# A hybrid encoder layer on one core: the first microseconds reworked (weights on ScalarE's DMA queue, low parts last, two token blocks open)

## The chip, the core and the metric

The kernel runs on one core of a Trainium2 chip. A core has TensorE (PE; its weight loads are shown apart as PEld), VectorE (DVE), ScalarE (ACT), GpSimd (POOL) and SyncE (SP). Each takes its instructions in the order in which the program lists them. SP issues transfers between the chip's main memory and the core; ACT can issue some too, on a queue of its own. Matmul results land in PSUM, everything else lives in SBUF. The metric is the time of one execution in microseconds (us) of the device, the median of several runs.

## The reference, cut to what matters

One layer for 512 tokens of width 1024, float32. Every projection is taken from the normalised input `h`:

```python
def rmsnorm(x, w):
    y = x * rsqrt(mean(x * x, axis=-1) + EPS)
    return y * w

h = rmsnorm(x, norm_w)                      # (512, 1024)
proj = h @ w_in + b_in                      # (1024, 11272) weights
(mq, mk, mv, mi, mf, mo, mz, sq, sk, sv, sz, gates) = split(proj)
y_m = mlstm(conv(mq, mk), mv, mi, mf) ...   # matrix memory, 4 heads
y_s = stick_breaking(norm(sq), norm(sk), sv) * silu(sz)   # 8 heads
merged = g_m * (y_m @ w_proj_m) + g_s * (y_s @ w_proj_s)
out = x + merged @ w_out
```

The change touches only how `h` and the first 512 columns of `sq` come about.

## The kernel before, in words

**Products in two parts.** To keep float32 accuracy, each operand of a matmul is split into a high part (rounded to the type `fp32r`) and a low part (what is left). A product is three matmuls: high x high, low x high, high x low (`mm3`). `hh` and `hl` are the high and low part of `h`, turned so that the model dimension lies on the partitions: eight k blocks of 128 rows, each with 512 tokens.

**Units.** The weights are worked off in units of 512 KB, 24 matmuls of 512 columns each. A unit is loaded by SP (`load`), split by ACT (high) and DVE (low), multiplied on PE and evacuated. The main loop over `c` (at the end of the code) writes out, for each unit, when later units are loaded and split (`ahead`), and between the two halves of a unit's matmuls the next piece of work of the attention heads. The order in which the program lists the instructions is the order on each engine; nothing reorders them.

**The first four units** (`sq`, 512 columns) are special. Unit i brings rows 256 i to 256 i + 255 of the weights, two k blocks. Their high parts `fh` (`f_w[k][0]`) and low parts `fl` (`f_w[k][1]`) for all eight k are made up front (`first_split`), and what the loop calls the matmuls of unit tb is the product of token block tb (128 tokens) with all eight k: 24 matmuls into one PSUM tile `f_ps[tb]`.

**The beginning.** SP issues, in this order: block 0 of x in two halves (`load_x(0)`), `norm_w`, the weights of units 0 and 1, block 1 of x, the weights of units 2 and 3, blocks 2 and 3 of x, and then many small rows (`load_vecs`). PE meanwhile multiplies zeros (`warm`, tile `idle`). `norm_vec` turns `norm_w`. `x_scale(tb)` squares a block on ACT with a running sum, makes the reciprocal root on POOL (a multiply-add and a power), and scales the block on DVE. `x_turn(tb)` transposes its eight 128 x 128 pieces on PE, four to a PSUM tile; DVE then makes `hh` (one instruction for four pieces) and `hl` (four instructions) from each tile. `first_split(0)` stands ahead of `x_turn(0)`, the splits of units 1 to 3 behind it; the low parts of units 1 and 3 are POOL's, those of 0 and 2 DVE's. In the loop, `x_turn(1)` and `x_turn(2)` stand between the halves of blocks 0 and 1, and `x_turn(3)` behind those of block 1. The evacuation of block tb (`qraw`, DVE) is at the start of step tb + 1, with four Squares on ACT behind it. Unit 4 is the first ordinary one; its first matmul has line 85.

Of the kernel before, what the change touches and what calls it, by code (L numbers as in the profile page):

```python
# [34 lines left out]
def tile_hybrid_layer(  # L35
# [58 lines left out]
    class Unit:  # L94
# [12 lines left out]
        def load(self, tag="stg"):  # L107
            self.st = blk(tag, shape=self.shape)
            nc.sync.dma_start(self.st, self.ap)
# [153 lines left out]
    def x_scale(tb):  # L263
        xs = tiny.tile([128, 4], F32, name="xs", bufs=2)
        ssq, r = xs[:, 0:2], xs[:, 2:3]
        xn = x_t[tb]
        junk = blk("om", BF, (D,), name="junk")
        if tb == 0:
            for i in range(2):
                c = slice(i * D // 2, (i + 1) * D // 2)  # L270
                nc.scalar.activation(junk[:, c], xn[:, c], AF.Square, accum_out=ssq[:, i:i + 1])
            nc.gpsimd.tensor_tensor(ssq[:, 0:1], ssq[:, 0:1], ssq[:, 1:2], op=OP.add)
        else:
            nc.scalar.activation(junk, xn, AF.Square, accum_out=ssq[:, 0:1])
        rstd(r, ssq[:, 0:1], D, EPS)
        nc.vector.tensor_scalar(xn, xn, r, None, op0=OP.mult)

    def x_turn(tb):
        ts = slice(tb * 128, (tb + 1) * 128)
        xn = x_t[tb]  # L280
        for g in range(2):
            ks = slice(4 * g, 4 * g + 4)
            tp = att_ps()
            for j in range(4):
                kt = g * 4 + j
                nc.tensor.transpose(tp[:, j * 128:(j + 1) * 128], xn[:, kt * 128:(kt + 1) * 128], ident)
            dh = hh[:, ks, ts]
            nc.vector.tensor_tensor(dh, tp.rearrange("p (k t) -> p k t", k=4),
                                    nw_t[:, ks].unsqueeze(2).to_broadcast([128, 4, 128]), op=OP.mult)
            for j in range(4):  # L290
                k = 4 * g + j
                nc.vector.scalar_tensor_tensor(hl[:, k, ts], tp[:, j * 128:(j + 1) * 128], nw_t[:, k:k + 1],
                                               hh[:, k, ts].bitcast(F32), op0=OP.mult, op1=OP.subtract)
# [592 lines left out]
    def first_split(i, low=None):  # L886
        u = units[i]
        for j in range(2):
            hi, lo = blk("qk", FR, name="fh"), blk("y", FR, name="fl")
            nc.scalar.activation(hi, u.st[:, j, :], AF.Copy)  # L890
            (low or nc.vector).tensor_tensor(lo, u.st[:, j, :], hi.bitcast(F32), op=OP.subtract)  # L891
            f_w.append((hi, lo))

    units[0].load()
    units[1].load()
# [16 lines left out]
    warm(9)  # L912
    norm_vec()
    x_scale(0)
    warm(2)
    first_split(0)
    x_turn(0)
    first_split(1, nc.gpsimd)
    x_scale(1)
    first_split(2)  # L920
    first_split(3, nc.gpsimd)

    f_ps = []

    def first_mm(tb):
        def mm(half):
            if half == 0:
                f_ps.append(dense_ps())
            for k in range(4 * half, 4 * half + 4):
                sh, sl = h_sta(k, tb)  # L930
                wh, wl = f_w[k]
                nc.tensor.matmul(f_ps[tb], sh, wh, start=k == 0, stop=False)  # L932
                nc.tensor.matmul(f_ps[tb], sl, wh, start=False, stop=False)  # L933
                nc.tensor.matmul(f_ps[tb], sh, wl, start=False, stop=k == KT - 1)  # L934
        return mm
# [44 lines left out]
    for c in range(N):  # L980
# [13 lines left out]
        if c < 2:  # L994
            x_turn(c + 1)
        if c == 0:
            x_scale(2)
            x_scale(3)
# [13 lines left out]
        if c == 1:  # L1012
            x_turn(3)
# [31 lines left out]
```

## Time and profile before

| | |
|---|---|
| median of 3 runs | 719.03 us (718.92 to 719.14) |
| the profiled execution | 720.13 us |
| its span, first to last instruction | 718.4 us |
| PE busy | 709.8 us, 99% of the span |
| DVE, ACT, POOL busy | 424.5, 315.8, 93.5 us |
| mean granted TensorE clock | 0.997 |

The profile shows one execution. Times in it count from the first instruction. Busy time of PE includes the modelled end of each pipelined matmul, so neighbours overlap in the list: of two matmuls that follow one another, the distance of the starts is the time that one takes. "Idle before" is the time an engine stood still ahead of an instruction, and the name behind the arrow is what ended it.

### The profile page before, as it was taken

To read this page: it belongs to the slowest core of one execution; us is meant where nothing else is said; L and a number is where in the kernel's file an instruction comes from. 1 tells how busy PE (TensorE), PEld (TensorE's weight loads), DVE (VectorE), ACT (ScalarE), POOL (GpSimd) and SP (SyncE) were. 2 spreads that over 40 slices of the span, in tenths; PEclk is the share of its full clock that TensorE was granted. 3 is DMA by queue.
4 is the path that set the end of the run, shared out by engine and by line. 5 is a ranking of instruction groups with operands and counts; after the bars stand their busy time and mean duration, and the time that the engine had idled before them with its cause. 6 is when DMAs were issued, how large, how long until landed. Compare 5 with 4: busy or idle time off the path is not lost.

```text
span 718.4 us, 9058 instructions
## 1 busy us (share of the span) xinstructions
PE 709.8 (99%) x3356; PEld 593.1 (83%) x3356; DVE 424.5 (59%) x663; ACT 315.8 (44%) x601; POOL 93.5 (13%) x235
## 2 busy tenths in 40 slices
PE   7999999999999999999999999999999999999997
PEld 5888888888888888888888888888888888888886
DVE  5837886656487568279944737994343254556441
ACT  5245364476255544244475534447554343222210
POOL 5422022253022112000001110000112000000000
PEclk9999999999999999999999999999999999999999
DMA  6433332233323222333332233333223333333621
GB/s 239 133 103 81 109 86 77 69 95 92 99 62 87 58 86 62 102 91 97 101 94 59 63 99 88 91 100 89 74 59 89 89 91 97 104 88 89 234 89 58
DMA packets 91475, 67.80 MB, mean 94 GB/s; under 512 B 3470, under 2 KB 77608, under 8 KB 91432
## 3 DMA queue, kind: packets, MB, share of 16 engines
q1 hardware_dynamic: 91432, 67.23, 32.8%
q8 instruction: 26, 0.43, 0.2%
q14 instruction: 17, 0.14, 0.1%
HBM read 65.12 MB, written 2.10 MB: 94 GB/s over the span
## 4 chain that ended last, share of the span: by engine, by line
PE 97%; DMA 1%; DVE 1%; POOL 0%; SPq 0%; issue 0%; ACT 0%; DVEq 0%
PE dps L85 28%; PE dps L87 27%; PE dps L86 27%; PE aps L86 2%; PE aps L87 2%; PE aps L85 2%; PE aps L440 1%; PE aps L382 1%; DMA stg<-in_w_in_dram 1%; PE dps L934 1%; PE dps L932 1%; PE dps L933 1%; PE aps L735 1%; PE aps L736 1%; PE aps L737 1%; DVE fl L891 0%
## 5 line engine op out<-in xcount | busy, mean ns | idle before, releaser
L91 DVE TENSOR_TENSOR wl<-stg,wh 128x1024 fp32r<-128x1024 f32 x108 | 132.3, 1225 | 140.3 <-ACT wh L90 139.9
L85 PE MATMUL dps<-hh,wh 128*128 128x512 f32 x448 | 175.8, 392 | 0.0
L86 PE MATMUL dps<-hl,wh 128*128 128x512 f32 x448 | 174.6, 390 | 0.0
L87 PE MATMUL dps<-hh,wl 128*128 128x512 f32 x448 | 174.6, 390 | 0.0
L90 ACT ACTIVATE wh<-stg 128x1024 fp32r<-128x1024 f32 x108 | 113.6, 1052 | 95.3 <-PE dps L87 58.6
L87 PEld LDWEIGHTS dps<-hh,wl 128*128 128x128 f32 x448 | 84.1, 188 | 17.7
L85 PEld LDWEIGHTS dps<-hh,wh 128*128 128x128 f32 x448 | 84.2, 188 | 17.5 <-issue 1.0
L86 PEld LDWEIGHTS dps<-hl,wh 128*128 128x128 f32 x448 | 84.2, 188 | 16.6
L85 PE MATMUL dps<-wh,hh 128*128 128x512 f32 x224 | 88.3, 394 | 0.0
L87 PE MATMUL dps<-wh,hl 128*128 128x512 f32 x224 | 87.4, 390 | 0.0
L86 PE MATMUL dps<-wl,hh 128*128 128x512 f32 x224 | 87.4, 390 | 0.0
L87 PEld LDWEIGHTS dps<-wh,hl 128*128 128x128 f32 x224 | 42.1, 188 | 8.9
L86 PEld LDWEIGHTS dps<-wl,hh 128*128 128x128 f32 x224 | 42.1, 188 | 8.2
L85 PEld LDWEIGHTS dps<-wh,hh 128*128 128x128 f32 x224 | 42.1, 188 | 8.2
L626 DVE SCALAR_TENSOR_TENSOR acc<-tmp,vec,acc 128x511 f32<-128x511 f32 (+2 forms) x48 | 36.0, 750 | 1.7
L629 ACT ACTIVATE tmp<-acc 128x512 f32<-128x512 f32 x16 | 10.1, 633 | 50.2 <-DVE acc L626 50.2
L415 DVE TENSOR_TENSOR_SCAN om<-om 128x512 f32<-128x512 f32 (+3 forms) x32 | 27.9, 871 | 6.3 <-POOL om L409 6.3
L409 POOL TENSOR_SCALAR_AFFINE_SELECT om<-om 128x128 f32<-128x128 f32 x32 | 12.1, 378 | 134.5 <-ACT om L407 134.5
L90 ACT ACTIVATE at_split<-aps 128x384 fp32r<-128x384 f32 (+1 forms) x24 | 11.8, 525 | 36.8 <-PE aps L440 36.8
L688 POOL TENSOR_SCALAR_AFFINE_SELECT w_all<-om 128x128 f32<-128x128 f32 x16 | 4.1, 293 | 168.9 <-DVE om L683 168.9
L91 DVE TENSOR_TENSOR at_split<-aps,at_split 128x384 fp32r<-128x384 f32 (+1 forms) x24 | 13.7, 599 | 19.8 <-ACT at_split L90 19.8
L86 PE MATMUL dps<-wl,mgh 128*128 128x512 f32 x64 | 24.9, 389 | 0.0
(239 smaller groups left out, 1170.6 us busy)
## 6 DMA issues: line engine op xcount, KB each, us to landing
stg<-in_w_in_dram SPq DMA_DIRECT2D x87, 512.0 KB, 3.7
stg<-in_w_proj_s_dram SPq DMA_DIRECT2D x8, 512.0 KB, 3.7
stg<-in_w_proj_m_dram SPq DMA_DIRECT2D x8, 512.0 KB, 3.6
stg<-in_w_out_dram SPq DMA_DIRECT2D x8, 512.0 KB, 3.7
brow<-in_b_in_dram SPq DMA_DIRECT2D x8, 256.0 KB, 4.2
xr<-in_x_dram SPq DMA_DIRECT2D x8, 256.0 KB, 5.7
out_dram<-xr SPq DMA_DIRECT2D x7, 256.0 KB, 2.3
x<-in_x_dram SPq DMA_DIRECT2D x3, 512.0 KB
```

Of the source, the lines that this page charges most:

```text
L85: nc.tensor.matmul(ps, ah, bh, start=first, stop=False)
L86: nc.tensor.matmul(ps, ah, bl, start=False, stop=False)
L87: nc.tensor.matmul(ps, al, bh, start=False, stop=last)
L90: nc.scalar.activation(hi, src, AF.Copy)
L91: nc.vector.tensor_tensor(lo, src, hi.bitcast(F32), op=OP.subtract)
L382: nc.tensor.transpose(tp[:, tb * 128:(tb + 1) * 128], self.raw[name][tb][:, hs], ident)
L409: nc.gpsimd.affine_select(out=om[:, ts], in_=om[:, ts], compare_op=OP.is_gt, fill=1.0, base=0, channel_multiplier=1, pattern=[[-1, 128]])
L415: nc.vector.tensor_tensor_scan(back, back, back, 1.0, op0=OP.mult, op1=OP.bypass)
L440: nc.tensor.transpose(tp[:, at + (i - j) * 128:at + (i - j + 1) * 128], a_t[i][:, j * 128:(j + 1) * 128], ident)
L626: nc.vector.scalar_tensor_tensor(acc[:, j:], t[:, 0:T - j], cw(3 - j, ch), acc[:, j:], op0=OP.mult, op1=OP.add)
L629: nc.scalar.activation(t, acc, AF.Sigmoid)
L735: nc.tensor.matmul(nm[:, 0:258], ph, vh, start=j == 0, stop=False)
```

## The change

- The weights of units 0 and 1 are loaded on ACT's queue instead of SP's.
- `first_split` becomes `first_high` (ACT) and `first_low` (DVE, all eight; none on POOL any more). All high parts are made ahead of the loop, the low parts of k 0 to 3 behind block 1's scale, those of k 4 to 7 in the loop's first step.
- `x_scale` is cut into `x_square` (ACT; its scale now holds the division by the width) and `x_scale` (POOL and DVE; for block 0 the scale is in two halves, and the sum of the two half sums is part of the multiply-add).
- `x_turn` no longer makes `hl` at once but returns two functions that do. For block 0 `hh` is made by DVE as before; for blocks 1 to 3 by ACT, eight instructions of 128 x 128 with a scale.
- The products are listed anew: `first_a` is the two with the weights' high part, all four k with `hh` and then all four with `hl`; `first_b` is the one with the low part. Block 0 takes `first_a` for all k, then come block 1's transposes, then `first_b` of block 0 for k 0 to 3, `first_a` of block 1 for k 0 to 3, and `first_b` of block 0 for k 4 to 7: two blocks are open at once. Block 1 goes on in the same manner around the transposes of block 2; blocks 2 and 3 take `first_a`, `first_b` for each half.
- `warm`: 8, 2 and 2 products of zeros, the last two behind block 0's transposes, instead of 9 and 2.

The number of matmuls for the result is the same.

```diff
--- before.py
+++ after.py
@@ -104,9 +104,9 @@
             self.slow = None
             self.heavy = False
 
-        def load(self, tag="stg"):
+        def load(self, tag="stg", by=None):
             self.st = blk(tag, shape=self.shape)
-            nc.sync.dma_start(self.st, self.ap)
+            (by or nc.sync).dma_start(self.st, self.ap)
 
         def split(self):
             self.wh = blk("wh", FR, self.shape)
@@ -260,37 +260,51 @@
         nc.gpsimd.tensor_scalar(dst, ssq, 1.0 / n, eps, op0=OP.mult, op1=OP.add)
         nc.gpsimd.tensor_tensor(dst, dst, mhalf[:, 0:dst.shape[1]], op=OP.pow)
 
-    def x_scale(tb):
+    def x_square(tb):
         xs = tiny.tile([128, 4], F32, name="xs", bufs=2)
-        ssq, r = xs[:, 0:2], xs[:, 2:3]
         xn = x_t[tb]
         junk = blk("om", BF, (D,), name="junk")
-        if tb == 0:
-            for i in range(2):
-                c = slice(i * D // 2, (i + 1) * D // 2)
-                nc.scalar.activation(junk[:, c], xn[:, c], AF.Square, accum_out=ssq[:, i:i + 1])
-            nc.gpsimd.tensor_tensor(ssq[:, 0:1], ssq[:, 0:1], ssq[:, 1:2], op=OP.add)
-        else:
-            nc.scalar.activation(junk, xn, AF.Square, accum_out=ssq[:, 0:1])
-        rstd(r, ssq[:, 0:1], D, EPS)
-        nc.vector.tensor_scalar(xn, xn, r, None, op0=OP.mult)
+        n = 2 if tb == 0 else 1
+        for i in range(n):
+            c = slice(i * D // n, (i + 1) * D // n)
+            nc.scalar.activation(junk[:, c], xn[:, c], AF.Square, scale=D ** -0.5, accum_out=xs[:, i:i + 1])
+        return xs
+
+    def x_scale(tb, xs):
+        xn = x_t[tb]
+        r = xs[:, 2:3]
+        n = 2 if tb == 0 else 1
+        nc.gpsimd.tensor_scalar(r, xs[:, 0:1], xs[:, 1:2] if tb == 0 else 0.0, EPS, op0=OP.add, op1=OP.add)
+        nc.gpsimd.tensor_tensor(r, r, mhalf[:, 0:1], op=OP.pow)
+        for i in range(n):
+            c = slice(i * D // n, (i + 1) * D // n)
+            nc.vector.tensor_scalar(xn[:, c], xn[:, c], r, None, op0=OP.mult)
 
     def x_turn(tb):
         ts = slice(tb * 128, (tb + 1) * 128)
         xn = x_t[tb]
+        low = []
         for g in range(2):
             ks = slice(4 * g, 4 * g + 4)
             tp = att_ps()
             for j in range(4):
                 kt = g * 4 + j
                 nc.tensor.transpose(tp[:, j * 128:(j + 1) * 128], xn[:, kt * 128:(kt + 1) * 128], ident)
-            dh = hh[:, ks, ts]
-            nc.vector.tensor_tensor(dh, tp.rearrange("p (k t) -> p k t", k=4),
-                                    nw_t[:, ks].unsqueeze(2).to_broadcast([128, 4, 128]), op=OP.mult)
-            for j in range(4):
-                k = 4 * g + j
-                nc.vector.scalar_tensor_tensor(hl[:, k, ts], tp[:, j * 128:(j + 1) * 128], nw_t[:, k:k + 1],
-                                               hh[:, k, ts].bitcast(F32), op0=OP.mult, op1=OP.subtract)
+            if tb == 0:
+                nc.vector.tensor_tensor(hh[:, ks, ts], tp.rearrange("p (k t) -> p k t", k=4),
+                                        nw_t[:, ks].unsqueeze(2).to_broadcast([128, 4, 128]), op=OP.mult)
+            else:
+                for j in range(4):
+                    k = 4 * g + j
+                    nc.scalar.activation(hh[:, k, ts], tp[:, j * 128:(j + 1) * 128], AF.Copy, scale=nw_t[:, k:k + 1])
+
+            def lows(g=g, tp=tp):
+                for j in range(4):
+                    k = 4 * g + j
+                    nc.vector.scalar_tensor_tensor(hl[:, k, ts], tp[:, j * 128:(j + 1) * 128], nw_t[:, k:k + 1],
+                                                   hh[:, k, ts].bitcast(F32), op0=OP.mult, op1=OP.subtract)
+            low.append(lows)
+        return low
 
     def bias_row(c0):
         b = blk("brow")
@@ -883,16 +897,18 @@
 
     f_w = []
 
-    def first_split(i, low=None):
-        u = units[i]
+    def first_high(i):
         for j in range(2):
             hi, lo = blk("qk", FR, name="fh"), blk("y", FR, name="fl")
-            nc.scalar.activation(hi, u.st[:, j, :], AF.Copy)
-            (low or nc.vector).tensor_tensor(lo, u.st[:, j, :], hi.bitcast(F32), op=OP.subtract)
+            nc.scalar.activation(hi, units[i].st[:, j, :], AF.Copy)
             f_w.append((hi, lo))
 
-    units[0].load()
-    units[1].load()
+    def first_low(k):
+        hi, lo = f_w[k]
+        nc.vector.tensor_tensor(lo, units[k // 2].st[:, k % 2, :], hi.bitcast(F32), op=OP.subtract)
+
+    units[0].load(by=nc.scalar)
+    units[1].load(by=nc.scalar)
     load_x(1)
     units[2].load()
     units[3].load("P5")
@@ -909,29 +925,57 @@
         for _ in range(n):
             nc.tensor.matmul(wp, idle[:, 0:128], idle, start=True, stop=True)
 
-    warm(9)
+    warm(8)
     norm_vec()
-    x_scale(0)
+    xs0 = x_square(0)
     warm(2)
-    first_split(0)
-    x_turn(0)
-    first_split(1, nc.gpsimd)
-    x_scale(1)
-    first_split(2)
-    first_split(3, nc.gpsimd)
-
-    f_ps = []
+    x_scale(0, xs0)
+    first_high(0)
+    first_high(1)
+    low0 = x_turn(0)
+    warm(2)
+    low0[0]()
+    xs1 = x_square(1)
+    first_high(2)
+    first_high(3)
+    low0[1]()
+    x_scale(1, xs1)
+    for k in range(4):
+        first_low(k)
+
+    f_ps = [None] * TB
+
+    def first_a(tb, ks):
+        if 0 in ks:
+            f_ps[tb] = dense_ps()
+        for p in range(2):
+            for k in ks:
+                nc.tensor.matmul(f_ps[tb], h_sta(k, tb)[p], f_w[k][0], start=p == 0 and k == 0, stop=False)
+
+    def first_b(tb, ks):
+        for k in ks:
+            nc.tensor.matmul(f_ps[tb], h_sta(k, tb)[0], f_w[k][1], start=False, stop=k == KT - 1)
+
+    lo_k, hi_k = range(4), range(4, 8)
 
     def first_mm(tb):
         def mm(half):
-            if half == 0:
-                f_ps.append(dense_ps())
-            for k in range(4 * half, 4 * half + 4):
-                sh, sl = h_sta(k, tb)
-                wh, wl = f_w[k]
-                nc.tensor.matmul(f_ps[tb], sh, wh, start=k == 0, stop=False)
-                nc.tensor.matmul(f_ps[tb], sl, wh, start=False, stop=False)
-                nc.tensor.matmul(f_ps[tb], sh, wl, start=False, stop=k == KT - 1)
+            if tb == 0 and half == 0:
+                first_a(0, lo_k)
+                first_a(0, hi_k)
+            elif tb == 0:
+                first_b(0, lo_k)
+                first_a(1, lo_k)
+                first_b(0, hi_k)
+            elif tb == 1 and half == 0:
+                first_a(1, hi_k)
+                first_b(1, lo_k)
+            elif tb == 1:
+                first_b(1, hi_k)
+            else:
+                ks = hi_k if half else lo_k
+                first_a(tb, ks)
+                first_b(tb, ks)
         return mm
 
     for tb in range(TB):
@@ -992,10 +1036,14 @@
         ahead(c)
         units[c].mm(0)
         if c < 2:
-            x_turn(c + 1)
+            low = x_turn(c + 1)
+            low[0]()
+            low[1]()
         if c == 0:
-            x_scale(2)
-            x_scale(3)
+            for k in hi_k:
+                first_low(k)
+            for tb in (2, 3):
+                x_scale(tb, x_square(tb))
             gates_fill()
         for g in list(act):
             if c in REST:
@@ -1010,7 +1058,8 @@
                 act.append(g)
         units[c].mm(1)
         if c == 1:
-            x_turn(3)
+            for fn in x_turn(3):
+                fn()
     now[0] = N
     units[N - 1].evac()
     assert not act and not pend and not later, (act, pend, later)
```

## Rows read from the trace of the kernel before

**Rows 1.** The page: busy us (share of the span) and count of instructions of each engine; and the chain of work that ended last, by engine.

```profile
PE 709.8 (99%) x3356; PEld 593.1 (83%) x3356; DVE 424.5 (59%) x663; ACT 315.8 (44%) x601; POOL 93.5 (13%) x235
...
PE 97%; DMA 1%; DVE 1%; POOL 0%; SPq 0%; issue 0%; ACT 0%; DVEq 0%
```

**Rows 2.** Windows: three stretches (us from the span's start). The columns are the stretch and its length, then busy us (and instructions) of PE, PEld, DVE, ACT and POOL, the granted TensorE clock, the DMA engines' busy share, GB/s.

```profile
8.50:10.60 2.10, 0.00 (x0) 0.00 (x0) 1.95 (x4) 1.83 (x5) 0.60 (x1) 1.00 1.05 408
10.60:11.60 1.00, 0.94 (x3) 0.74 (x4) 1.00 (x5) 1.00 (x2) 1.00 (x2) 0.59 1.07 432
...
38.00:700.00 662.00, 662.00 (x3154) 555.35 (x3154) 394.19 (x598) 299.42 (x562) 75.54 (x202) 1.00 0.32 91
```

**Rows 3.** The timeline of PE, 0 to 41 us. The columns are start us, us, engine, line, operation, out<-in, shapes, count, and in brackets the idle time before with what ended it.

```profile
1.50 4.21 PE L910 MATMUL dps<-idle 128*128 128x512 f32 x9 [1.50 <-DVE idle L905]
...
6.95 1.28 PE L286 MATMUL aps<-ident,x 128*128 128x128 f32 x8
10.66 0.64 PE L932 MATMUL dps<-fh,hh 128*128 128x512 f32 x1 [2.43 <-DVE hh L288]
...
14.11 0.44 PE L934 MATMUL dps<-fl,hh 128*128 128x512 f32 x1
...
17.68 0.50 PE L934 MATMUL dps<-fl,hh 128*128 128x512 f32 x1 [0.41 <-DVE fl L891]
...
25.74 1.03 PE L286 MATMUL aps<-ident,x 128*128 128x128 f32 x8
...
32.07 0.25 PE L236 MATMUL aps<-ident,v_rows 98*128 98x98 f32 x1
...
38.04 0.39 PE L85 MATMUL dps<-wh,hh 128*128 128x512 f32 x1
...
40.53 0.39 PE L87 MATMUL dps<-wh,hl 128*128 128x512 f32 x1
```

**Rows 4.** The timeline of ACT, 0 to 13 us, in the same columns.

```profile
0.78 1.28 ACT L271 ACT_TABLE_LOAD   x1 [0.78 <-PEq L1032]
3.49 0.63 ACT L271 ACTIVATE junk<-x 128x512 bf16<-128x512 f32 x1 [1.42 <-DMA x<-in_x_dram]
...
4.12 0.63 ACT L271 ACTIVATE junk<-x 128x512 bf16<-128x512 f32 x1
...
7.96 1.15 ACT L890 ACTIVATE fh<-stg 128x512 fp32r<-128x512 f32 x2 [3.12 <-DMA stg<-in_w_in_dram]
9.29 1.15 ACT L890 ACTIVATE fh<-stg 128x512 fp32r<-128x512 f32 x2 [0.19 <-DMA stg<-in_w_in_dram]
10.53 1.06 ACT L274 ACTIVATE junk<-x 128x1024 bf16<-128x1024 f32 x1
```

**Rows 5.** The timeline of DVE, 6 to 18 us, in the same columns.

```profile
6.14 0.75 DVE L276 TENSOR_SCALAR x<-x,xs 128x1024 f32<-128x1024 f32 x1
8.62 1.29 DVE L891 TENSOR_TENSOR fl<-stg,fh 128x512 fp32r<-128x512 f32 x2 [1.72 <-ACT fh L890]
9.83 0.68 DVE L288 TENSOR_TENSOR hh<-aps,nw_t 128x512 fp32r<-128x512 f32 x1
10.55 1.13 DVE L292 SCALAR_TENSOR_TENSOR hl<-aps,nw_t,hh 128x128 fp32r<-128x128 f32 x4
...
13.47 0.75 DVE L276 TENSOR_SCALAR x<-x,xs 128x1024 f32<-128x1024 f32 x1
14.14 3.49 DVE L891 TENSOR_TENSOR fl<-stg,fh 128x512 fp32r<-128x512 f32 x2
```

**Rows 6.** The timeline of POOL, 10 to 17 us, in the same columns.

```profile
10.00 2.51 POOL L891 TENSOR_TENSOR fl<-stg,fh 128x512 fp32r<-128x512 f32 x2 [3.96 <-ACT fh L890]
12.60 0.19 POOL L260 TENSOR_SCALAR xs<-xs 128x1 f32<-128x1 f32 x1
12.87 0.56 POOL L261 TENSOR_TENSOR xs<-xs,mhalf 128x1 f32<-128x1 f32 x1
13.76 3.32 POOL L891 TENSOR_TENSOR fl<-P,fh 128x512 fp32r<-128x512 f32 x2 [0.33 <-ACT fh L890]
```

**Rows 7.** Windows of the first eight us, in the columns of rows 2; the last column is read here.

```profile
1.50:3.00 1.50, 1.50 (x4) 1.21 (x5) 0.00 (x0) 0.56 (x1) 0.00 (x0) 1.00 0.69 234
3.00:4.00 1.00, 1.00 (x4) 0.81 (x3) 0.00 (x0) 0.51 (x1) 0.00 (x0) 1.00 0.88 223
4.00:5.00 1.00, 1.00 (x3) 0.79 (x3) 0.00 (x0) 0.84 (x4) 0.08 (x1) 1.00 0.77 216
5.00:6.00 1.00, 1.00 (x4) 0.34 (x2) 0.06 (x1) 0.00 (x0) 0.83 (x3) 1.00 1.08 377
6.00:7.00 1.00, 1.00 (x3) 0.39 (x3) 0.86 (x2) 0.00 (x0) 0.04 (x1) 1.00 1.03 371
7.00:8.00 1.00, 1.00 (x9) 0.99 (x8) 0.00 (x0) 0.04 (x1) 0.00 (x0) 1.00 1.03 416
```

**Rows 8.** The timeline of SP's DMA issues: start us, us that the issues took, line, tensor, count.

```profile
0.79 0.84 SPq L193 DMA_DIRECT2D x<-in_x_dram  x2
...
2.08 0.90 SPq L109 DMA_DIRECT2D stg<-in_w_in_dram  x2
```

**Rows 9.** Groups of ACT's instructions by line and shape: count | busy us, mean ns of one | idle before.

```profile
L411 ACT ACTIVATE a_all<-aps,rq 128x128 f32<-128x128 f32 x8 | 3.0, 377 | 0.0
...
L801 ACT ACT_TABLE_LOAD x2 | 2.6, 1283 | 0.0
```

## The prediction

> **What bounds the kernel now.** I read the page's busy shares and its chain first: TensorE (PE) is busy nearly the whole span, and the chain that ended last is almost all matmuls [rows 1]. Next I read the windows: from 38 us to 700 us PE has no idle time at all, at a granted clock of 1.00 [rows 2]. So a change at the beginning is worth exactly what it takes off the moment at which PE starts the first matmul of unit 4, line 85, at 38.04 us [rows 3], as long as nothing later is starved. Everything below is about that moment.
>
> PE's timeline to 38 us shows three losses [rows 3]. PE waits 2.43 us before the first product at 10.66, for hh. Its first eight products are 0.43 us apart ((14.11 - 10.66)/8), where later ones are 0.226 us apart (11 steps from 38.04 to 40.53): the granted clock fell to half at 10.7 [rows 2], the 1.2 GHz level, after PE had stood idle from 8.23 to 10.66. That costs 8 x 0.205 = 1.64 us. And at 17.68 it waits 0.41 us for fl. The rest is work: 24 products with 8 transposes take 32.07 - 25.74 = 6.33 us, of which 24 x 0.226 = 5.42, so 0.9 us for a block of transposes.
>
> The engines' own timelines tell why. DVE could have made hh soon after the transposes ended at 8.23, but its list has the low parts of unit 0 first (8.62, 1.29 us), which wait for ACT's copy, which waits for the weights, seen at 7.96 [rows 4, 5]. The second weights are seen at 9.29. POOL's low parts (10.00 and 13.76) hold back the two small operations for block 1's scale, so that DVE scales block 1 at 13.47 [rows 5, 6]; and the pair of splits that DVE makes beside POOL's takes 3.49 us, against 1.29 us alone.
>
> **Where the bytes are.** The windows' rates add up to 0.351 + 0.223 + 0.216 + 0.377 + 0.371 = 1.54 MB by 7.0 us [rows 7]. Block 0 (x0) and the first two weights (w0, w1), 0.524 MB each, are complete in bytes at about 3.8, 5.7 and 7.1 us, but ACT can start on them at 4.12, 7.96 and 9.29 [rows 4]: 0.3, 2.2 and 2.2 us later. A load counts when its slowest part is in. Around 3 to 5 us the rate is half of what it is from 5 us on: the issues of w0 and w1 at 2.08 come too late to fill it [rows 7, 8].
>
> **The change, part by part.**
>
> *Weights on ACT's queue.* ACT issues w0 and w1 at about 0.8 us instead of SP at 2.08; an issue costs some 0.42 us (0.84 for two, [rows 8]), so the table load of 1.28 us moves from 0.78 to about 1.6 and ends at 2.9, still before x0 is there at 3.49: hidden. The data path was already at 0.37 to 0.42 MB/us when one queue fed it [rows 7], so a second queue can fill the hole but not raise the rate. x0 then shares with w0: 1.05 MB are through at 3.0 + 0.70/0.4 = 4.75, and x0's second half is seen at 5.1 instead of 4.12 (lag 0.3). w1 shares with what SP has next, block 1 (x1, 0.524 MB): before it is complete 2.10 MB must have moved, or 2.36 MB if the larger pieces of x1 pass first and half of the third weights go with it. That is at 3.0 + 1.75/0.4 = 7.4 to 8.0 us, plus a lag of 0.3 to 2.2 us: **w1 is seen between 7.7 and 10.2**; I take the middle, 9.0, since w0's and w1's lags were both at the upper end with one queue and nothing shows which end two queues give. That is hardly earlier than today's 9.29. The Trainium skill, "DMA: Bandwidth & Descriptors", section "Issuing engines are not separate DMA queues", speaks against this part: loads of several issuers share the same engines and interleave, and only issue time is saved; no row here has two queues in flight. By that rule w1 is at the 9.0 of the sum, without it at 6 (rival A).
>
> *Order of the list.* hh now stands ahead of every low part on DVE, and the scale of block 0 is cut in two, so the transposes start at about 7.4 (x0 at 5.1, Squares to 5.9, POOL 0.84 without the add, half a scale 0.4) and the first product at about 9.0 instead of 10.66. With it go the long idle stretch, the slow clock and the waits for POOL. All that would be 1.64 + 0.41 + some 1.6 us, if the products could follow at once. They cannot, and this is what decides.
>
> *What ACT must do first.* ACT's list is now: copies of w0, copies of w1, Square of block 1, copies of w2 and w3, then block 1's hh, eight pieces. From w1's landing: two copies 1.1, the Square with its read 1.2 (10.53 to the next instruction), four copies 2.1 [rows 4], with 0.1 of handing over: the last high part is there at w1 + 4.5 = 13.5. PE, in order, then has product 7 and the four with hl, 5 x 0.23 = 1.2, and only then block 1's transposes: 0.8 to the first four's result, 0.4 for ACT's first piece. The trace has no such piece; the nearest row is the 128x128 Sigmoid from PSUM with a pointer scale, 377 ns [rows 9], and DVE's 128x128 from PSUM is 1.13 us for four [rows 5]. Between 0.26 and 0.38 us each I take 0.29, since neighbours on ACT overlap by some 0.09 (two copies of 0.62 in 1.15 busy, [rows 4]). So the first piece of block 1 is there at w1 + 6.9 = 15.9.
>
> *What DVE must do.* Four splits that POOL had are now DVE's: 4 x 0.62 = 2.5 us more; it saves 3.49 - 1.29 = 2.2 us beside the idle POOL and 1.4 us for block 1's hh. Its first four splits follow the scale of block 1, which now waits for ACT's Square instead of for POOL: w1 + 3.3 = 12.3, splits 13.0 to 15.5, so 0.4 us ahead of 15.9: hidden. Then hl of block 1, paced by ACT's pieces: 8 x 0.29 = 2.3, to 18.2; then splits 4 to 7: 3 x 0.62 + 0.69 = 2.6, to 20.8. PE's fourth product with them starts at 20.9. (Before, the last wait ended at 17.68, but with 14 fewer products done.)
>
> *What is left then.* That product and 64 more, 65 x 0.226 = 14.7; two blocks of transposes 1.8; the vectors' transposes and their neighbours 0.5: 17.0 us without a wait. Blocks 2 and 3 have hh and hl by 30 us, before PE needs them; unit 4's loads need their buffers free at about 15 to 21 and its products come at 38. End: 20.9 + 17.0 = **37.9 against 38.04**, a gain of 0.1 us. The two idle products moved and the one added hide before the first transposes or in the wait for ACT; without that cover two would cost 0.85 us.
>
> The sum is made against the profiled execution: 720.13 us, of which 718.4 is span. The median of the runs is 1.10 below the profiled time; I carry the difference over: 719.03 - 0.1 = 718.9. The end moves with w1 one for one from 9.0 on: at 10.2 it is 39.1 (+1.1). Earlier than that other landings (w3, x0) begin to count: at 7.7 about 36.8 (-1.3). So the likeliest case's own range is 717.7 to 720.1.
>
> **Rivals.**
>
> A. *The loads do not hold each other up*, or the lag vanishes with the early issue: x0 at 4.1, w1 at about 6, w3 at 9. For it: the hole at 3 to 5 us. Against it: the rate that stands at 0.37 to 0.42 MB/us whenever several loads are queued. The last high part is then at about 10.4, transposes of block 1 at 11.9, but DVE's list binds: hh to 8.4, hl to 10.6, scale to 11.4, four splits to 13.9, hl to 16.0, splits to 18.5; end 18.6 + 17.0 = 35.6 to 36.5 with x0 half delayed: 716.6 to 717.5.
>
> B. *Slower by the clock.* Between 18.7 and 20.9 PE has four products for over two us, since each waits for its split. Before, a near-empty stretch of 2.43 us was followed by 3.4 us at half clock [rows 2, 3]. If the clock falls there at 21, from where PE is the bound, eight products take 0.43 us: 1.64 us, so 37.9 + 1.6 = 39.5, 720.5. It decides as soon as the granted clock is 0.5 anywhere after 21 us. Against it: PE stays at work in 40% of that stretch, and in none of 8.23 to 10.66.
>
> C. *ACT issues after its table load*, or the shared path is worse than the bound (x0 held back by w0's slow parts to 7, w1 after 10.5). Then w0 leaves at 2.1 beside x1: w1 near 10.7, end 39.6, 720.6. Against it: the load that later stands at a Sigmoid's own line (801) rather than earlier [rows 9]; so I expect it behind the two issues. The Trainium skill, "ScalarE: Activation LUTs", "Step-by-step: what each stage is for", also puts a table load right in front of the activation that needs it.
>
> **How the numbers follow.** The forecast (w1 at 7.7 to 10.2, sharing as worked out) has 0.52, A 0.30, B 0.09, C 0.09. 0.2% is 1.4 us, about what a measurement of this kernel can tell from no change. The forecast lies inside that; A falls beyond it with nearly all its weight, B and C too. Faster 0.30, same 0.52, slower 0.18. The range takes A's better part and B's price up to the last tenth on each side: 717.0 to 720.5.
>
> **What would show it.** In the profile after: two issues on ACT at 0.8 and the table load behind them; x0's second Square at about 5; the third fh at about 9 (this one number decides between forecast, A and C); first product near 9; no clock of 0.5 from 11 us on; DVE without idle time worth naming from 13 to 21; POOL without splits; the last wait of PE before a fl at 20 to 21; the first line 85 product at 37.9. The prediction is wrong if w1 lands before 7.5 with DVE's list shorter than I count, if ACT's small pieces cost well over 0.29 us each, or if PE waits again in blocks 2 and 3.

## The result, and the profile after

The changed kernel takes 720.58 us (median of 7 runs, 720.36 to 722.1), the kernel before, run beside it, 718.92 (7 runs, 718.61 to 719.15): ratio 1.0028, 95% interval 1.0016 to 1.0040. It is slower by 1.7 us, where no measurable change was forecast. The profiled execution of after is its median one: 720.58 us, span 718.7.

The page's busy shares answer [rows 1]: PE is as full as before.

```profile
PE 709.9 (99%) x3357; PEld 592.6 (82%) x3357; DVE 421.0 (59%) x662; ACT 321.5 (45%) x625; POOL 88.9 (12%) x230
```

From the first matmul of unit 4 (line 85) to the last matmul both traces need the same 675.73 us (713.77 - 38.04 and 714.47 - 38.74), so the beginning decides, as argued from [rows 2] (the end of the span helps after by 0.40 us, see below). The timeline of PE after, in the columns of [rows 3]:

```profile
6.84 0.20 PE L217 MATMUL aps<-ident,v_rows 8*128 8x8 f32 x1 [1.55 <-DMA v_rows<-in_norm_w_dram]
...
8.48 1.32 PE L292 MATMUL aps<-ident,x 128*128 128x128 f32 x8 [0.78 <-DVE x L281]
9.45 1.20 PE L926 MATMUL dps<-idle 128*128 128x512 f32 x2
10.46 1.91 PE L953 MATMUL dps<-fh,hh 128*128 128x512 f32 x4
...
15.12 1.03 PE L292 MATMUL aps<-ident,x 128*128 128x128 f32 x8
...
19.75 2.31 PE L957 MATMUL dps<-fl,hh 128*128 128x512 f32 x4 [0.85 <-DVE fl L908]
21.89 1.09 PE L953 MATMUL dps<-fh,hh 128*128 128x512 f32 x4
...
27.23 1.17 PE L953 MATMUL dps<-fh,hh 128*128 128x512 f32 x4
...
38.74 0.39 PE L85 MATMUL dps<-wh,hh 128*128 128x512 f32 x1
```

The first product starts at 10.46, hardly before the 10.66 of [rows 3]. The four products at 19.75 take 2.31 us instead of 1.07 behind 0.85 of idle time: PE waits for each of the last four low parts. Line 85 is at 38.74, against the forecast 37.9. The timelines of ACT and DVE show the two ends of that wait; they answer [rows 4, 5] (of [rows 6] only the small operations on xs are left, POOL makes no split):

```profile
0.78 0.99 ACTq L109 DMA_DIRECT2D stg<-in_w_in_dram  x2
1.80 1.28 ACT L270 ACT_TABLE_LOAD   x1 [1.80 <-issue]
...
6.11 0.63 ACT L270 ACTIVATE junk<-x 128x512 bf16<-128x512 f32 x1 [1.56 <-DMA x<-in_x_dram]
...
8.76 1.15 ACT L903 ACTIVATE fh<-stg 128x512 fp32r<-128x512 f32 x2 [0.89 <-DMA stg<-in_w_in_dram]
...
11.89 1.14 ACT L903 ACTIVATE fh<-P 128x512 fp32r<-128x512 f32 x2
15.76 2.17 ACT L299 ACTIVATE hh<-aps,nw_t 128x128 fp32r<-128x128 f32 x8 [2.72 <-PE aps L292]
```

```profile
13.18 2.49 DVE L908 TENSOR_TENSOR fl<-stg,fh 128x512 fp32r<-128x512 f32 x4
16.93 2.16 DVE L304 SCALAR_TENSOR_TENSOR hl<-aps,nw_t,hh 128x128 fp32r<-128x128 f32 x8 [1.27 <-ACT hh L299]
19.01 1.28 DVE L908 TENSOR_TENSOR fl<-stg,fh 128x512 fp32r<-128x512 f32 x2
20.21 1.29 DVE L908 TENSOR_TENSOR fl<-P,fh 128x512 fp32r<-128x512 f32 x2
...
22.61 1.41 DVE L281 TENSOR_SCALAR x<-x,xs 128x1024 f32<-128x1024 f32 x1 [0.45 <-POOL xs L278]
23.95 0.67 DVE L342 TENSOR_TENSOR qraw<-dps,brow 128x512 f32<-128x512 f32 x1
```

x0's second half is seen at 6.11 instead of 4.12, the second weights (w1) at 8.76. ACT's pieces for block 1 come 0.26 us apart from 15.76 on, but DVE starts hl only at 16.93, after the fourth, and then runs through at its own pace. The chain of waits up to PE's last wait, cut to some of its larger pieces (start us, us, what), puts it in order:

```profile
1.21 4.88 DMA x<-in_x_dram
...
9.80 0.85 PE dps L926 x2
10.66 4.63 PE dps L953 x16
...
16.52 1.41 ACT hh L299 x5
...
19.09 1.72 DVE fl L908 x3
```

It begins with x, not with the weights, and PE's own 16 products are on it: PE never waits between 10.46 and 15.28.

### The profile page after: what moved, and what is told of

Its sections match the earlier page's. It is cut to its first block, busy times and chain, and to the rows that moved or that the text cites. A ratio compares the mean times of both kernels' runs of the same rounds, so it can differ in the third digit from the quotient of the medians.

```text
span 718.7 us, 9073 instructions
## 1 busy us (share of the span) xinstructions
PE 709.9 (99%) x3357; PEld 592.6 (82%) x3357; DVE 421.0 (59%) x662; ACT 321.5 (45%) x625; POOL 88.9 (12%) x230
## 4 chain that ended last, share of the span: by engine, by line
PE 97%; DMA 1%; DVE 1%; ACT 0%; POOL 0%; issue 0%; SPq 0%; DVEq 0%
PE dps L85 27%; PE dps L86 27%; PE dps L87 27%; PE aps L86 2%; PE aps L87 2%; PE aps L85 2%; PE dps L953 2%; PE aps L454 1%; PE aps L396 1%; PE dps L957 1%; DMA x<-in_x_dram 1%; PE aps L749 1%; PE aps L750 1%; PE aps L751 1%; PE aps L292 0%; PE aps L776 0%
## 5 line engine op out<-in xcount | busy, mean ns | idle before, releaser
L90 ACT ACTIVATE at_split<-aps 128x384 fp32r<-128x384 f32 (+1 forms) x24 | 11.8, 526 | 36.8 <-PE aps L454 36.8
L85 PE MATMUL dps<-yh,wh 128*128 128x512 f32 x64 | 24.9, 389 | 0.0
```

What stands on the lines that cost most here:

```text
L85: nc.tensor.matmul(ps, ah, bh, start=first, stop=False)
L90: nc.scalar.activation(hi, src, AF.Copy)
```

## The experiments

Each ratio is that of a kernel to the kernel before, run beside it on the same chip, with its 95% interval; it is not always the quotient of the two medians. The interval reaches some 0.6 us to either side, so a difference of less than about 0.9 us between two experiments isn't shown by their times alone; what is said of it goes by their traces. In the six traces with the weights on ACT's queue x0's second half is seen at 6.00 to 6.13 us and w1 at 8.76 to 9.45; in the eight with SP's, x0's second half at 4.08 to 4.25 and w1 at 7.87 to 8.78, but 9.29 in the profile of before.

**e1: the changed kernel, weights back on SP's queue.**

```diff
-    units[0].load(by=nc.scalar)
-    units[1].load(by=nc.scalar)
+    units[0].load()
+    units[1].load()
```

> The changed kernel with one part undone: the first two weights are again issued by SP, in the old place. Theory Q (the shared path: x's first block held back by the weights beside it, second Square at 6.11 us instead of 4.12, is what the change loses): block 0 is there at 4.1 again, the first product comes some 1.5 us earlier than 10.46, and the run is 1 to 2 us faster than the changed kernel's 720.6. Theory L (the list: the second weights' landing, then ACT's copies, Square, copies and small pieces, then DVE's four splits): the third copy starts at 9.3 as in the kernel before instead of 8.76, and line 85 starts 0.5 us later than the 38.74 of the changed kernel: 0.5 us slower than it.

Measured: 719.99 us (before 719.17), ratio 1.0014 [1.0005, 1.0023]. It stands 0.8 us above its own runs of before, the changed kernel 1.7 above its own: half of the loss is back, less than Theory Q said, and Theory L had the wrong sign. The timeline of PE in e1:

```profile
11.29 1.02 PE L953 MATMUL dps<-fh,hh 128*128 128x512 f32 x2 [0.54 <-ACT fh L903]
...
19.00 2.30 PE L957 MATMUL dps<-fl,hh 128*128 128x512 f32 x4 [0.84 <-DVE fl L908]
```

The first product comes at 8.26, 2.2 us earlier than in after, but the later ones wait for high parts, and the wait for the low parts of k 4 to 7 stands as it was (DVE stands idle for 1.50 us ahead of block 1's hl); line 85 is at 38.28. So the rest of the change, the order of the list and the work given to DVE, costs by itself.

**e2: the kernel before, with only the weights on ACT's queue.**

```diff
-    units[0].load()
-    units[1].load()
+    units[0].load(by=nc.scalar)
+    units[1].load(by=nc.scalar)
```

> The kernel before with one part of the change alone: the first two weights on ACT's queue. Theory Q: x's block 0 lands at 6 us, the transposes start near 9 instead of 6.95, and the run is 1 to 2 us slower than the kernel before. Theory L: block 0 is not what the kernel before waits for (hh waits for the splits behind the weights); the second weights are 0.5 us earlier, so between 0.5 us faster and 0.3 us slower than the kernel before.

Measured: 720.34 us (before 719.17), 1.0015 [1.0007, 1.0024]: the medians are 1.17 apart, as Theory Q said. ACT's timeline in e2 has both loads late:

```profile
6.00 0.63 ACT L271 ACTIVATE junk<-x 128x512 bf16<-128x512 f32 x1 [1.46 <-DMA x<-in_x_dram]
...
9.45 1.15 ACT L890 ACTIVATE fh<-stg 128x512 fp32r<-128x512 f32 x2 [1.69 <-DMA stg<-in_w_in_dram]
```

But it is not x0 that comes last here. In the old order the chain up to PE's last wait, as the profile of before shows it (start us, us, what), begins with w1:

```profile
2.52 6.75 DMA stg<-in_w_in_dram
...
9.29 0.64 ACT fh L890
...
10.00 2.51 POOL fl L891 x2
...
14.14 3.50 DVE fl L891 x2
```

POOL's two small operations for block 1's scale stand behind its low parts of w1. In e2 w1 is seen at 9.45 instead of the 8.38 of e4 below, which has the old order and one queue, and POOL's low parts start at 10.16 instead of 9.09. The timelines of POOL and DVE in e2:

```profile
10.16 2.52 POOL L891 TENSOR_TENSOR fl<-stg,fh 128x512 fp32r<-128x512 f32 x2 [2.24 <-ACT fh L890]
```

```profile
13.63 1.77 DVE L276 TENSOR_SCALAR x<-x,xs 128x1024 f32<-128x1024 f32 x1 [0.20 <-POOL xs L261]
```

The two paths meet at DVE's scale of block 1: the one from x0, through DVE's own list, is there 0.20 us before the one from w1. So Theory Q's number came out, with w1 in x0's place by a hair.

Both parts of the change cost: about 1.2 us the queue alone and 0.8 the rest alone. That the two add up to more than the 1.7 of both together is within the intervals.

**e3: the changed kernel, two of every four low parts on POOL again.**

```diff
-        nc.vector.tensor_tensor(lo, ...
+        (nc.gpsimd if k % 4 > 1 else nc.vector).tensor_tensor(lo, ...
```

> The changed kernel with the low parts of k 2, 3, 6 and 7 given back to POOL, at their new place in the order. Theory L (DVE's list sets the end): the last two splits leave DVE's chain, 2 x 0.62 us behind block 1's hl, so line 85 starts 1.2 us earlier than 38.74 and the time is 1.2 us under the changed kernel's. Theory Q or a clock theory: no change beyond 0.3 us, since landings and the clock are not touched; DVE's own splits may slow beside POOL's to 1.7 us each, which by L is hidden up to the wait of 1.27 us for block 1's hh.

Measured: 720.80 us, 1.0022 [1.0013, 1.0031]; line 85 at 38.99. No gain, by Theory L 1.2 us were due. DVE's list is shorter, but what it does beside POOL takes longer; the timelines of DVE and POOL in e3:

```profile
13.85 3.46 DVE L908 TENSOR_TENSOR fl<-stg,fh 128x512 fp32r<-128x512 f32 x2
```

```profile
12.09 2.99 POOL L908 TENSOR_TENSOR fl<-stg,fh 128x512 fp32r<-128x512 f32 x2
```

The same pair takes DVE 3.46 us beside POOL's and 1.28 alone, as in [rows 5]. PE's last wait ended 0.45 us earlier than in after (21.44 against 21.89), yet block 2's hh on ACT started later (26.67 against 26.27). Something behind the wait binds too.

**e4: the kernel before, with eight products of zeros where PE stood idle ahead of its first product.**

```diff
     x_turn(0)
+    warm(8)
     first_split(1, nc.gpsimd)
```

> The kernel before with eight products of zeros behind block 0's transposes, where PE stood idle from 8.23 to 10.66 us. They do no work for the result. Theory C (the granted clock's low stretch costs its 1.64 us in the kernel before and comes and goes from run to run): the stretch at 0.5 from 10.7 us disappears and the run is up to 1.6 us faster in those executions that had it. Theory L: the first products are faster but PE then waits longer for the splits, which end at 17.6 whatever the clock, so the time is the same within 0.3 us.

Measured: 719.34 us (before 719.17), 1.0001 [0.9992, 1.0010]. Windows and PE timeline of e4:

```profile
10.60:14.20 3.60, 2.88 (x17) 2.19 (x16) 3.01 (x7) 3.16 (x7) 3.13 (x4) 1.00 1.00 348
```

```profile
13.39 1.09 PE L286 MATMUL aps<-ident,x 128*128 128x128 f32 x8 [0.72 <-DVE x L276]
16.77 0.50 PE L935 MATMUL dps<-fl,hh 128*128 128x512 f32 x1 [0.73 <-DVE fl L891]
```

The granted clock stays at 1.00, where it had been at the 1.2 GHz level [rows 2], the products are faster, and PE waits 1.45 us for block 1's x and the low parts where it waited 0.41 [rows 3]. In the profiled execution of before the slow stretch cost nothing: its products are not on the chain shown under e2, and the 0.41 us of waiting stands behind them. The equal medians say less: of the 33 executions of before beside e4, 26 have a mean clock of 0.999 or more and so hardly such a stretch. This trace also has the weights seen at 6.55 and 8.38 and line 85 at 37.14: 0.9 us earlier than in the profile of before, though the two medians agree.

**e5: the changed kernel, block 1's transposes between the halves of block 0's products, not behind all 16.**

```diff
             if tb == 0 and half == 0:
                 first_a(0, lo_k)
-                first_a(0, hi_k)
             elif tb == 0:
+                first_a(0, hi_k)
                 first_b(0, lo_k)
```

> The changed kernel with block 1's transposes moved ahead of the eight products of block 0 with the high k (one line moved, the work is the same). Theory P (PE's own order holds back block 1: its data are scaled at 13.2 us but its transposes stand behind products that end at 15.1): transposes at 13.3, ACT's fourth piece at 15.2 instead of 16.9, DVE's hl right behind its first four splits at 15.7 instead of 16.93, its last split 1.2 us earlier, line 85 at 37.5: 1.2 us faster than the changed kernel's 720.6. Theory D (DVE's list itself or the late block 0 is the whole loss): within 0.3 us of the changed kernel.

Measured: 720.91 us (before 719.04), 1.0027 [1.0016, 1.0039]. The last low part came earlier: the products behind it start at 21.10 instead of 21.89. But the gain is lost at block 2, at the same moment as in after, and line 85 is at 39.10, not at the 37.5 of Theory P; PE in e5:

```profile
27.20 1.28 PE L953 MATMUL dps<-fh,hh 128*128 128x512 f32 x4 [0.53 <-ACT hh L299]
```

**e6: e5 with the weights on SP's queue** (the edits of e5 and e1 together).

> The same move, with the first two weights on SP's queue as in the run before. Theory P: in that run block 1 was scaled at 12.3 us and turned at 14.4; now turned at 12.3, ACT's fourth piece at 14.2, DVE without the idle 1.5 us from 14.7, last split at 19.4 instead of 20.7, line 85 at 36.8 instead of 38.3: 1.4 us faster than that run (720.0) and 0.5 us faster than the kernel before (719.2). Theory D: 720.0 again.

Measured: 719.55 us, 1.0008 [1.0000, 1.0017], line 85 at 37.29, 1.0 us earlier than in e1 but short of the 36.8 expected; PE again waits 0.52 us for block 2's hh.

**e9: e5, with DVE's evacuation of block 0 ahead of its scales of blocks 2 and 3.** ACT's list has four Squares of `qraw` ahead of block 2's hh, and `qraw` stands on DVE behind both scales (23.95 in after, 24.48 in e5), which wait for POOL's roots.

```diff
+        if c == 1:
+            x_mul(2, xs23[0])
+            x_mul(3, xs23[1])
...
-            for tb in (2, 3):
-                x_scale(tb, x_square(tb))
+            xs23 = [x_square(2), x_square(3)]
+            x_root(2, xs23[0])
+            x_root(3, xs23[1])
```

(`x_root` is the POOL half of `x_scale`, `x_mul` the DVE half; the first three lines stand behind the evacuation.)

> The changed kernel with block 1's transposes ahead of block 0's high k, as tried before, and in addition DVE's scales of blocks 2 and 3 listed behind the evacuation of block 0 instead of ahead of it (their roots on POOL stay where they were). Theory S (a second chain: the two scales wait for POOL's slow roots, hold back the evacuation, and with it ACT's four Squares and block 2's hh): evacuation at 21.4 instead of 24.5, ACT's first piece of block 2 at about 24.5 instead of 26.8, no wait of PE at block 2, line 85 at 38.0 to 38.2 instead of the 38.7 to 39.1 of the changed kernel and of the run with the move alone: 0.8 us faster than that run's 720.9. If no second chain binds: as that run, within 0.2 us.

Measured: 719.95 us (before 718.99), 1.0012 [1.0004, 1.0021]; e5 stood 1.87 above its before, e9 0.96. POOL, DVE and ACT in e9:

```profile
18.19 2.94 POOL L276 TENSOR_TENSOR xs<-xs,mhalf 128x1 f32<-128x1 f32 x1
```

```profile
18.23 1.28 DVE L915 TENSOR_TENSOR fl<-stg,fh 128x512 fp32r<-128x512 f32 x2
...
21.50 0.69 DVE L349 TENSOR_TENSOR qraw<-dps,brow 128x512 f32<-128x512 f32 x1 [0.78 <-DMA brow<-in_b_in_dram]
```

```profile
24.75 4.23 ACT L306 ACTIVATE hh<-aps,nw_t 128x128 fp32r<-128x128 f32 x16 [0.82 <-PE aps L299]
```

Block 2's hh starts at 24.75 instead of 26.80 in e5, PE doesn't wait for it, and line 85 is at 38.23 instead of 39.10. That is the second chain: POOL's roots late, scales late, `qraw`, Squares, hh. It had been hidden just behind the first.

**e7: the changed kernel, six products of zeros inside the wait for the low parts of k 4 to 7.**

```diff
         for k in ks:
+            if tb == 0 and k > 3:
+                warm(3 if k == 4 else 1)
             nc.tensor.matmul(f_ps[tb], h_sta(k, tb)[0], f_w[k][1], ...
```

> The changed kernel with six products of zeros where PE waits for the last four splits (three ahead of the first, one ahead of each of the others; together 1.4 us of the 2.1 us that it waits). They do no work for the result. Theory C (in some executions the granted clock falls after this wait and costs 1.6 us: two of the seven executions had mean clocks of 0.994 and 0.995 and spans of 720.0 and 720.2): the long executions disappear, all spans lie between 718.3 and 719.0, the fastest stay where they are. If the long ones come from late landings, they are as frequent as before.

Measured: 720.61 us, 1.0023 [1.0015, 1.0032]. Of after's seven executions two are long, with spans of 720.0 and 720.2 at a mean clock of 0.995 and 0.994. With the zeros the long ones remain, four of eleven with spans of 719.2 to 719.8, but all at a clock of 1.00; those at 0.997 to 0.998 have 718.3 to 718.8. So a low clock behind that wait (rival B) isn't needed for a long execution; whether it made after's two longer than e7's four isn't shown. What makes the long ones stays open: in two profiles of long executions of other kernels, before's and e11's (717.9), the first weights are seen at 7.96 and 7.45 where the other six with one queue have 6.10 to 6.55, but no long one of after or e7 was profiled.

**e8: e6, with the first low part ahead of block 1's scale**, on DVE where it otherwise waits for POOL's root.

```diff
+    first_low(0)
     x_scale(1, xs1)
-    for k in range(4):
+    for k in range(1, 4):
         first_low(k)
```

> As the run with the move and the weights on SP's queue, and the first of DVE's splits moved ahead of block 1's scale, into the 0.7 us in which DVE waits for that scale's root. Theory P: the chain behind it is DVE's list without a gap, so 0.6 us more: line 85 at 36.2, span 716.3, time 718.0 to 718.2, faster than both kernels. If ACT's pieces (fourth at 14.2) or PE bind by then, 0.1 us or nothing more than without it.

Measured: 718.94 us, 1.0001 [0.9992, 1.0010], but in two groups: six spans of 715.6 to 717.0 at a mean clock of 0.999 or more, five of 717.5 to 717.8 at 0.996 to 0.997. The profiled one is of the first, with line 85 at 36.11 and 1.86 us of idle time left in PE's timeline:

```profile
12.40 1.09 PE L292 MATMUL aps<-ident,x 128*128 128x128 f32 x8 [1.86 <-DVE x L281]
```

**e10: e8 with e9's move as well**, and **e11: e10 with six products of zeros** in the wait ahead of block 1's transposes (the line added in e12 below).

> The run with the weights on SP's queue, block 1 turned early and one split moved, and in addition the scales of blocks 2 and 3 behind the evacuation of block 0. Theory S: the last products of block 0 end at 19.2 as before and PE has no further wait; that run had none in its profile, so the profile moves little (line 85 at 36.1), but executions with late loads lose less. 0 to 0.5 us faster than 718.9.

> As the run before it, with six products of zeros in the wait of 1.9 us ahead of block 1's transposes. They do no work for the result. Theory C (a low stretch of the granted clock after that wait makes the long executions of the run with one split moved: mean clock 0.996 or 0.997 with spans of 717.5 to 717.8 beside 715.6 to 717.0): no execution with a mean clock under 0.998, median 0.5 to 1 us lower than without the zeros, at 718.0 to 718.4. If late loads make them: as without the zeros.

Measured: 719.43 us, 1.0007 [0.9998, 1.0015], and 719.34, 1.0001 [0.9992, 1.0010]. Both miss. With the weights on SP's queue DVE comes to `qraw` before the bias row is there; DVE and PE in e10:

```profile
21.76 0.69 DVE L349 TENSOR_TENSOR qraw<-dps,brow 128x512 f32<-128x512 f32 x1 [2.60 <-DMA brow<-in_b_in_dram]
```

```profile
23.23 1.09 PE L299 MATMUL aps<-ident,x 128*128 128x128 f32 x8 [0.78 <-DVE x L284]
```

The scale of block 2, now behind `qraw`, waits with it. The move that gained 0.9 us with the weights on ACT's queue is a new wait with them on SP's.

**e12: e8 with the six zeros alone.**

```diff
             if tb == 0 and half == 0:
                 first_a(0, lo_k)
+                warm(6)
```

> This is e8 (weights on SP's queue, block 1's transposes between the halves of block 0's products, the first low parts ahead of block 1's scale) with six products of zeros behind the first eight products of block 0, where PE otherwise stands idle until block 1 is scaled; the scales of blocks 2 and 3 stay where e8 has them. The executions of e8 fell into two groups: spans of 715.6 to 717.0 with a mean granted clock of 0.999 or more, and spans of 717.5 to 717.8 with 0.996 to 0.997. Theory K (the low clock of the early stretch makes e8's long executions): no execution with a clock under 0.998, spans of 715.6 to 717.0, a median of 718.0 to 718.5, 0.6 to 1.0 faster than the kernel before. Theory L (late landings make both the long executions and, by PE's idle time, the low clock): clocks of 0.998 or more throughout, but spans as in e8 up to 717.8, median 718.9, no difference from the kernel before. If the zeros stand in the way of block 1's transposes (6 x 0.43 = 2.6 us at half clock against about 1.9 us of waiting): up to 0.7 slower than e8, 719.6.

Measured: 718.17 us (11 runs, 717.86 to 719.2), before 718.81 (14 runs, 718.45 to 719.24); ratio 0.9992 [0.9983, 1.0001]. All eleven executions have a mean clock of 0.999 or more, and ten have spans of 715.9 to 716.5. PE in e12:

```profile
10.35 1.55 PE L926 MATMUL dps<-idle 128*128 128x512 f32 x6
...
36.43 0.39 PE L85 MATMUL dps<-wh,hh 128*128 128x512 f32 x1
```

With the zeros the low clock is gone, and of e8's group at 717.5 to 717.8 one execution is left (717.4): here, where PE has little slack behind the wait, the low clock cost about a microsecond, which is Theory K. The size is rough, since e8 and e12 were not run beside each other. Against their own runs of before, the changed kernel stands 1.66 us above and e12 0.64 below. Its interval reaches just past 1, so "not slower" is shown and "faster" is likely.

## Why the prediction was wrong

Forecast and result are 1.69 us apart: 0.84 of line 85 (38.74 against 37.9), 1.10 that was carried over from the profile to the median, 0.15 more time outside the span (1.88 against 1.73), less 0.40 by which after's span ends sooner behind its last matmul.

**The baseline.** The largest part, 1.10 us, is the step "I carry the difference over": it failed. The profiled execution of before was a late one: of some hundred runs of before beside the experiments only two had a span of 718.4 or more, and the middle is 717.3. The lags of 2.2 us in [rows 4] belonged to that execution (weights seen at 7.96 and 9.29; with the old order and queue e4 had 6.55 and 8.38). No ordinary execution of before was profiled, but line 85 is at 37.14 in e4, and the usual span less the 680.4 us from line 85 to the end (718.4 - 38.04) gives 36.9. So a forecast of 37.9 for after was a loss of 0.8 to 1.0 us, taken for a gain of 0.1. The median of the runs, 1.10 below the profile, was the sign that stood in view.

**Weights on ACT's queue.** That a second queue doesn't raise the rate held: in after it is 0.37 to 0.42 MB/us from 4 us on, as in before from 5 us on. The bytes ahead of that, and how the loads share them, came out otherwise. The sum took 0.4 MB/us from 3 us on and let x0 share with w0; the windows of after:

```profile
3.00:4.00 1.00, 1.00 (x4) 0.81 (x3) 0.00 (x0) 0.26 (x2) 0.00 (x0) 1.00 0.88 258
4.00:5.00 1.00, 1.00 (x4) 0.47 (x2) 0.00 (x0) 0.55 (x2) 0.00 (x0) 1.00 1.01 369
```

The hole of [rows 7] was filled only from 4 us on (0.369 against 0.216). Between 3 and 4 the rate was 0.258, and up to 3 us 0.246 MB had moved (1.5 x 0.164), where the sum took the 0.351 of before; all six traces with two queues have less there (0.21 to 0.27) than the eight with one (0.34 to 0.38). Of what moved from 3 to 5 us, four fifths were ACT's; the queues of after in that stretch (packets, MB, share of the 16 engines; q10 is ACT's, q1 SP's):

```profile
q10 hardware_dynamic: 262, 0.51, 78.2%
q1 hardware_dynamic: 65, 0.11, 15.9%
```

SP's queue, in which the rest of x0 stands, got 0.11 MB in 2 us, so x0 is seen at 6.11, not 5.1. Why ACT's queue got so much more isn't shown. What w0 may have gained, ACT couldn't use: its copies stand behind x0's Square and begin at 6.74.

That w1 would land at 9.0 was nearly right (8.76), but that this is "hardly earlier than today's 9.29" was not: it is later than usual, 7.87 to 8.78 in the other seven traces with one queue. In after w1 did not decide: the last high part was there at 13.03, the products reached block 1's transposes only at 15.12, because they began at 10.46. That the first piece of block 1 began at 15.76, so close to the 15.9 at which the sum has it done, was luck: the sum came there over w1 and ACT's copies, the trace over x0 and PE's own products.

The zeros counted as hidden were not wholly so: the two behind block 0's transposes are on the chain of waits for 0.85 us. They held PE up by at most 0.6 us, since hh's first half was ready at 9.86 and the first product began at 10.46. They ran in a stretch in which the granted clock is at the 1.2 GHz level, behind PE's waits for `norm_w` and x (1.55 and 0.78 us idle); from 22 us on it is 1.00:

```profile
9.20:12.60 3.40, 3.40 (x12) 2.73 (x11) 3.40 (x11) 3.40 (x8) 0.80 (x2) 0.50 1.05 418
...
22.00:38.70 16.70, 16.70 (x83) 13.75 (x82) 10.62 (x29) 9.81 (x37) 8.24 (x13) 1.00 0.24 77
```

The rule of the Trainium skill weighed in the prediction ("DMA: Bandwidth & Descriptors", "Issuing engines are not separate DMA queues") agrees with these rows: the two queues' packets share the same 16 engines, and the rate did not rise.

**What DVE must do.** The step "hl of block 1, paced by ACT's pieces ... to 18.2" failed: DVE waited for four pieces, not one (16.93), and ended at 19.09, splits at 21.50, the fourth product at 21.55 instead of 20.9. That is 0.65 of the 0.84 us at line 85. That DVE has no idle time between 13 and 21 was wrong by the same 1.27 us.

**What is left then.** 17.0 us forecast, 17.19 measured (38.74 - 21.55). Blocks 2 and 3 had their last hh at 30.48 and their last hl at 31.65, not by 30 us; "before PE needs them" held in after by a hair: where PE comes there 0.8 us earlier (e5), it waits 0.53.

**The clock.** The 1.64 us that the prediction read out of [rows 3] as a loss of before was no loss (e4): behind it stood a wait that did not depend on it, and most executions of before hardly have the stretch. So there was less to gain than it said.

**Rivals.** A (loads don't hold each other up) is out, by x0. B is out for the median execution, whose clock is 1.00 behind the wait; for the long ones it stays open: e7 shows that long ones come without it. C comes nearest in time, 720.6, and that is luck: its end came from w1 near 10.7, where w1 is at 8.76, and ACT does issue ahead of its table load (0.78, 1.80). Right in it is that x0 is held back, to 6.1, short of its 7.

## What to carry to other kernels

Before landing times are taken from a profile, set its time against the runs: 1.1 us above a median whose runs lie 0.2 apart says that this execution is late, and that its waits are not the usual ones. When the path is full, an earlier issue on a second queue is paid for by what the first queue has on its way: here x0, which the new order waits for, and w1, which the old one waits for. Where several chains end within a microsecond of each other, moving one shows the next: the gains of e3 and e5 at one place went at another, and only the version that left the queue alone, cut the first chain and filled its wait (e12) likely came out below the start.

## What the runs showed of the hardware

DVE and POOL hold each other up. In e3, with splits on both, DVE's pair took 3.46 us instead of 1.28. POOL's small operations are held up too: its power on 128 numbers took 0.56 us [rows 6] and 2.94 beside DVE's splits in e9, which were not slower for it (1.28). The Trainium skill, "SBUF — State Buffer", "SBUF: two separate sides", describes a pair of ports that DVE and GpSimd lock against each other, which agrees; in e9 POOL's operation came through only with the end of all four of DVE's splits (21.13 and 20.72).

With work waiting on two DMA queues, the share of each was far from even: 0.51 MB on ACT's and 0.11 on SP's from 3 to 5 us in after.

DVE starts work on ACT's pieces in groups of four in these traces, though each piece has its own instruction. The records of after have a wait for ACT ahead of the first of each four hl only, so this is how the program waits, and no limit of the engine is shown. No run tried a wait for each piece.

A low clock can be free or paid: a stretch of it cost nothing in the profiled execution of before (e4), and about 1 us in e8 (e12).
